# Six buffers for a matmul kernel's split weights, each at its own byte offset from the operand tiles

## The chip, the cores and the metric

The kernel runs on one core of one Trainium2 chip, in one launch. The metric is the time of that core in microseconds (us), as the median of three runs. Times of single instructions are in nanoseconds (ns).

## The reference

One decoder layer over 512 tokens with 2048 features, in float32:

```
mod = silu(c) @ w_ada + b_ada                  # six vectors of 2048
h   = rmsnorm(x, g_mix) * (1 + sc1) + sh1
proj = h @ w_in                                # 2048 x 11344, split in eleven parts
y_a = stick_breaking_attention(q_a, k_a, v_a) @ w_a
y_b = dsa_attention(rope(q_b), rope(k_b), v_b, rope(qi), rope(ki), wi) @ w_b
x   = x + (1 + gt1) * ((sigmoid(g_a) * y_a + sigmoid(g_b) * y_b) @ w_o)
h   = rmsnorm(x, g_ffn) * (1 + sc2) + sh2
u   = causal_conv3(h @ w_up)                   # 2048 x 11264
x   = x + (1 + gt2) * ((silu(u_a) * u_b) @ w_down)
return rmsnorm(x, g_final)
```

Nearly all of the arithmetic is in the products with w_in, w_o, w_up and w_down.

## The kernel before

**A product in three matmuls.** TensorE (PE) multiplies here in a reduced float32 format. To keep float32 accuracy each matrix is held as a high part (the value rounded to that format) and a low part (the rest). `mm3` (lines 142 to 145) makes one product out of three matmuls, high by high (L143), high by low (L144), low by high (L145), into one accumulator in PSUM. A weight tile of 128x1024 comes from memory into one of eight `raw` buffers (`load`). `parts` then splits it: ScalarE (ACT) writes the high part `wh` (L133), VectorE (DVE) writes the low part `wl` (L135). There are three `wh` and three `wl` buffers, and each tile takes the next of its three. `split` (L162, L164) does the same for the operands, which stay for long in the 62 slots `F` of 2048 bytes per partition.

**Two kinds of operand in a matmul.** Each matmul has a stationary operand, 128 columns that an LDWEIGHTS brings into the array beforehand, and a moving operand that is streamed through it, here 256 or 512 columns. The trace writes a matmul as out<-moving,stationary. So `acc<-F,wh 128x256` streams half of an `F` tile through a slice of `wh`, and `att<-wh,F 128x512` streams half of `wh` through a slice of an `F` tile.

**The stages**, with their time in the profile:
- up to about 108 us: most of the indexer's queries, `w_qi`, with `F` moving, 512 columns. Beside it DVE multiplies the first `w_ada` tiles with c. For the first two rounds of this loop `ada_half` borrows two `wl` and two `wh` buffers as landing place.
- to 190 us: `w_va`, with `wh` and `wl` moving; to 237 us a tail of 80 columns (`w_tail`, slices of 80 instead of 128 stationary columns) and three more blocks.
- to 824 us: 31 `unit`s of `w_x`. A unit is one step of Strassen's scheme for a pair of output tiles: seven products of 24 matmuls each, 256 columns, `F` moving and `wh` or `wl` stationary. DVE forms the sums of weight tiles (L233, L237, L275).
- to 1266 us: both attentions, with `w_vb`, `w_a` and `w_b` filled in; to 1445 us `w_o` in units.
- to 2294 us: `w_up`, three blocks plain and 41 units; then `w_down` with `wh` and `wl` moving, 512 columns. Its last stage takes weights that were split into `F` slots ahead of time, so both of its operands are `F` tiles.

**What sets the order.** The program is written with a tile framework. It allots a buffer when a tile is asked for, and a scheduler orders each engine's instructions by dependencies and by when it expects buffers to come free. Each engine then works through its own list and waits only on semaphores. SyncE's queue (SP) issues the weight loads in the order in which it has them.

**Where the buffers lie.** The pool lays tiles of different names one behind the other, in the order in which they are first asked for, each rounded up to a multiple of 32 bytes. In the built program the `F` slots begin at 26912 bytes and lie 2048 bytes apart, so every one begins 288 bytes past a multiple of 2048. The six `wl` and `wh` buffers lie 4096 apart and begin 352 bytes past such a multiple: all six are 64 bytes further on than the operand tiles. The 64 bytes are the small tile `c_col`, which happens to come first in between. A stationary slice of 128 columns is 512 bytes long, and half of an `F` tile 1024, so that the distance between a weight slice and an operand is 64 bytes modulo 512 in all these matmuls.

Of the kernel before, what the change touches and what calls it, by code (L numbers as in the profile page):

```python
# [10 lines left out]
F32 = mybir.dt.float32  # L11
F32R = mybir.dt.float32r
# [64 lines left out]
def block_kernel(ctx: ExitStack, tc: tile.TileContext, A: dict, out: bass.AP):  # L77
# [7 lines left out]
    def nm(s):  # L85
        counter[0] += 1
        return f"{s}_{counter[0]}"

    def t2k(tag, bufs, dt=F32, w=S):
        return sb.tile([P, w], dt, tag=tag, bufs=bufs, name=nm(tag))  # L90

    def slot(dt=F32):

        return t2k("F", SLOTS, dt)
# [14 lines left out]
    stt = nc.vector.scalar_tensor_tensor  # L109


    const = sb.tile([P, 5, P], F32, tag="const", name="const")
    ident, ones, negones, negtri, causal = (const[:, i, :] for i in range(5))
    vec = sb.tile([P, 96 + 2 * KT], F32, tag="vec", name="vec")
# [2 lines left out]
    g_mix, g_ffn = (vec[:, 96 + i * KT : 96 + (i + 1) * KT] for i in range(2))  # L117
    mask = sb.tile([P, 2, P], BF16, tag="mask", name="mask")
    cw = sb.tile([P, 2 * NJ, 4], F32, tag="cw", name="cw")
    eps = sb.tile([P, 1], F32, tag="eps", name="eps")  # L120
    nc.vector.memset(eps, EPS)


    def load(src, w=1024):
# [3 lines left out]

    pins = {}

    def parts(raw, w=1024):
        wh = t2k("wh", 3, F32R, w)
        pins["wh"] = act(wh, raw, AF.Copy)  # L133
        wl = t2k("wl", 3, F32R, w)
        pins["wl"] = tt(wl, raw, wh.bitcast(F32), ALU.subtract)  # L135
        return wh, wl

# [142 lines left out]
        return c1, c2  # L280


    macc = sb.tile([P, 96, 2], F32, tag="macc", name="macc")
    mod = sb.tile([P, 96], F32, tag="mod", name="mod")
    amp = sb.tile([P, 2, KT], F32, tag="amp", name="amp")

    def ada_half(cb, t, half, tag=("raw", 8)):
        raw = t2k(*tag, w=1024)
        nc.sync.dma_start(raw, A["w_ada"][t * P : (t + 1) * P, half * 1024 : (half + 1) * 1024])
        return stt(raw, raw, 1.0, cb[half], ALU.mult, ALU.mult, accum_out=macc[:, t, half : half + 1])  # L290
# [33 lines left out]
        return cb  # L324

    cb = c_spread()
    c_col = sb.tile([P, KT], F32, tag="c_col", name="c_col")
    nc.scalar.dma_start(c_col, A["c_col"])
    act(c_col, c_col, AF.Silu)

# [1 line left out]
    def rms(squares, blocks=range(NQB), bank=outs):  # L332

        total = bank()
        at = slice(blocks[0] * P, (blocks[-1] + 1) * P)
        for b in blocks:
            for i, t in enumerate(squares):
                mm(total[:, b : b + 1], t[:, b * P : (b + 1) * P], ones[:, :1], start=b == blocks[0] and i == 0,
                   stop=i == len(squares) - 1, skip_group_check=True)
        r = sb.tile([P, NQB], F32, tag="r", bufs=2, name=nm("r"))  # L340
        rb = r[:, blocks[0] : blocks[-1] + 1]
        act(rb, total[:, blocks[0] : blocks[-1] + 1], AF.Sqrt, scale=1.0 / D, bias=eps)
        nc.vector.reciprocal(rb, rb)
        wide = t2k("T", 2)
        for b in blocks:
            ts(wide[:, b * P : (b + 1) * P], ident, r[:, b : b + 1], None, ALU.mult)
        yield
        out = bank()
        mm(out[:, at], ones, wide[:, at], start=True, stop=True)
        yield out  # L350
# [16 lines left out]
    for k in range(KT):  # L367
        if k == 6:
            past = t2k("w", 2)[:, :P]
            with behind(pins["load"]):  # L370
                nc.sync.dma_start(const, A["consts"][:, :5])
                nc.sync.dma_start(past, A["consts"][:, 5])
            nc.gpsimd.tensor_copy(mask[:, 0, :], ident)
            nc.gpsimd.tensor_copy(mask[:, 1, :], past)
        t = KT + k
        for half in range(2):
            ada_half(cb, t, half, {0: ("wl", 3), 1: ("wh", 3)}.get(k, ("raw", 8)))
        if not k:
            total = next_x()
        x = xt[k]  # L380
        if k == KT - 1:
            norm = rms([total])
            next(norm)
        ada_end(t, t + 1)
        stt(amp[:, 0, k : k + 1], mod[:, t : t + 1], 1.0, g_mix[:, k : k + 1], ALU.add, ALU.mult)
        h0 = slot(F32R), slot(F32R)
        act(h0[0], x, AF.Copy, scale=amp[:, 0, k : k + 1])
        stt(h0[1], x, amp[:, 0, k : k + 1], h0[0].bitcast(F32), ALU.mult, ALU.subtract)  # L388
        w = prep(A["w_qi"][k], NQ * P)
        for j in range(NQ):  # L390
            mm3(qi_ps[j], cols(w, j), h0, k == 0, k == KT - 1)
            if k == KT - 1 and j == 0:
                rstd = t2k("T", 2)
                act(rstd, next(norm), AF.Copy)
        for _ in range(2 if k == 8 else 1):
            if len(xt) < KT:
                total = next_x()
# [91 lines left out]

    def rope_tables():  # L490
        f0, f1, f2, f3, f123, f23, fr = _turn_parts()
        inv = sb.tile([64, 1], F32, tag="inv", name="inv")
        nc.scalar.dma_start(inv, A["inv_freq"])
        pos = t2k("T", 2, I32)[:64]
        nc.scalar.dma_start(pos, A["positions"].to_broadcast([64, S]))
        turn = [t2k("w", 2)[:64] for _ in range(2)]

        def nearest(o, i, step):
            m = 1.5 * 2.0**23 * step
            ts(o, i, m, m, ALU.add, ALU.subtract)  # L500

        for half in range(2):
            at = slice(half * HALF, (half + 1) * HALF)
            q1, q2 = (t[:, at] for t in turn)
            tmp = sb.tile([P, 5 * HALF], F32, tag="soft", name=nm("soft"))[:64]
            ang, a2, a1, a0, rn = (tmp[:, i * HALF : (i + 1) * HALF] for i in range(5))
            nc.vector.tensor_copy(ang, pos[:, at])
            ts(ang, ang, inv, None, ALU.mult)
            nearest(a2, ang, 2.0**20)
            tt(ang, ang, a2, ALU.subtract)  # L510
            yield
            nearest(a1, ang, 2.0**8)
            tt(ang, ang, a1, ALU.subtract)
            nearest(a0, ang, 2.0**-4)
            tt(ang, ang, a0, ALU.subtract)
            small = ang
            ts(small, ang, fr, None, ALU.mult)
            yield
            stt(small, a0, f123, small, ALU.mult, ALU.add)
            stt(small, a1, f23, small, ALU.mult, ALU.add)  # L520
            stt(small, a2, f3, small, ALU.mult, ALU.add)
            ts(q1, a1, f0, None, ALU.mult)
            stt(q1, a2, f1, q1, ALU.mult, ALU.add)
            yield
            nearest(rn, q1, 1.0)
            tt(q1, q1, rn, ALU.subtract)
            ts(q2, a1, f1, None, ALU.mult)
            stt(q2, a2, f2, q2, ALU.mult, ALU.add)
            nearest(rn, q2, 1.0)
            tt(q2, q2, rn, ALU.subtract)  # L530
            yield
            stt(q1, a0, f0, q1, ALU.mult, ALU.add)
            tt(q1, q1, q2, ALU.add)
            nearest(rn, q1, 1.0)
            tt(q1, q1, rn, ALU.subtract)
            tt(q1, q1, small, ALU.add)
            yield
            nearest(rn, q1, 1.0)
            tt(q2, q1, rn, ALU.subtract)
            ts(q1, q2, 0.25, None, ALU.add)  # L540
            nearest(rn, q1, 1.0)
            tt(q1, q1, rn, ALU.subtract)
            yield
        TWO_PI = float(np.nextafter(np.float32(2 * np.pi), np.float32(0)))
        q1, q2 = turn
        for n, step in enumerate((64, 32)):
            o = t2k("raw", 8, w=1024)
            for i in range(P // step):
                at = slice(step * i, step * i + step)
                act(o[at, :S], q1[:step], AF.Sin, scale=TWO_PI)  # L550
                act(o[at, S:], q2[:step], AF.Sin, scale=TWO_PI if i % 2 else -TWO_PI)
                if i % 2:
                    yield
            save(rope_d[n], o)
# [459 lines left out]
    def norm_late(c1, c2):  # L1014
# [1 line left out]
        c, sq = (c1, c2), (t2k("ta", 2), t2k("sp", 2))  # L1016
        total, rstd = att(), outs()
        wide = t2k("T", 2)
        r = sb.tile([P, NQB], F32, tag="r", bufs=2, name=nm("r"))

        def add_up(t, blocks, first=False):
            for b in blocks:
# [415 lines left out]
        return [fetch(x1t[:, t, b * S : (b + 1) * S]) for b in range(2, 4)]  # L1438

    def finish_tokens(t, xs, s):  # L1440
        r = sb.tile([P, NQB], F32, tag="r", bufs=2, name=nm("r"))
        tt(r[:, :2], s[:, :2], s[:, 2:], ALU.add)
        tt(r[:, 2:3], r[:, :1], r[:, 1:2], ALU.add)
        act(r[:, 3:], r[:, 2:3], AF.Sqrt, scale=1.0 / D, bias=eps)
        nc.vector.reciprocal(r[:, 3:], r[:, 3:])
        for b, x in enumerate(xs):
            if t == NQB - 1 and b < 2:
                act(x, x, AF.Copy, scale=r[:, 3:])
            else:
                stt(x, x, r[:, 3:], g_row[b], ALU.mult, ALU.mult)  # L1450
            nc.sync.dma_start(out[t][:, b * S : (b + 1) * S], x)
# [136 lines left out]
```

## Time and profile before

| | |
|---|---|
| three runs | 2782.76, 2783.45, 2783.63 us |
| median | 2783.45 us |
| profiled execution, its own time | 2759.24 us |
| its span, first to last instruction | 2757.5 us |
| granted TensorE clock, mean | 0.995 |
| ACT busy | 1450.7 us (53%) |
| DMA: bytes moved, mean rate | 550.08 MB, 199 GB/s |
| largest group of DVE: `wl` (L135) | 792 instructions, 952.6 us |

The profiled execution is 24.2 us shorter than the median of the runs. A row of a group of instructions gives how many there were, for how long the engine worked on them, the mean duration of one, and how long the engine stood idle before them. Matmuls overlap in the pipeline: a matmul of 256 columns is shown with some 280 ns, but the next one starts after about 113 ns. What counts for the time is the distance from start to start, called the pace here. It is read from the starts in the timeline, or from the count of matmuls in a window without idle time.

### The profile page before, as it was taken

Reading aid. Unit: us, or ns where it says so; the run is one execution under the profiler, and the core shown is the slowest. Engines: PE = TensorE matmul, PEld = TensorE weight load, DVE = VectorE, ACT = ScalarE, POOL = GpSimd, SP = SyncE. Lnnn points to the kernel's source line nnn. Section 1 sums busy time; section 2 is a strip of 40 time slices with the busy share of each in tenths; the row PEclk is TensorE's granted clock in tenths of the full one; section 3 lists DMA queues with packets and bytes.
Section 4 is the critical chain, followed back from the end, with each engine's and each line's share of the span. In section 5 each row is a group of like instructions: output and inputs, shape, how many; then the busy total and the mean of one; then the engine's idle time right before and its main releaser. Section 6 shows DMA issues by size and latency. Waiting matters only on the chain.

```text
span 2757.5 us, 47708 instructions
## 1 busy us (share of the span) xinstructions
PE 2697.6 (98%) x18704; PEld 2457.7 (89%) x18704; DVE 2411.3 (87%) x3452; ACT 1450.7 (53%) x2045; POOL 315.3 (11%) x519
## 2 busy tenths in 40 slices
PE   8999999999999999999999999999999999999997
PEld 6779999999998777879999999999999998887876
DVE  8978979988887899889879999999999997888886
ACT  4444454455556655434557555555555555546452
POOL 0010000000012011111230000000000000002122
PEclk9999999999999999999999999999999999999998
DMA  9973456756567467865783566666666446569786
GB/s 348 354 254 122 156 181 195 232 176 188 166 195 238 133 206 243 279 213 174 233 269 108 179 176 178 187 177 184 176 179 182 130 131 219 151 176 245 193 256 196
DMA packets 164189, 550.08 MB, mean 199 GB/s; under 512 B 21414, under 2 KB 21798, under 8 KB 163964
## 3 DMA queue, kind: packets, MB, share of 16 engines
q1 hardware_dynamic: 116220, 405.34, 45.9%
q0 software_dynamic: 47152, 141.30, 18.4%
q8 instruction: 147, 2.41, 0.4%
q14 instruction: 78, 0.64, 0.1%
q10 hardware_dynamic: 592, 0.39, 0.1%
HBM read 453.71 MB, written 89.83 MB: 197 GB/s over the span
## 4 chain that ended last, share of the span: by engine, by line
PE 67%; DVE 8%; DMA 5%; issue 4%; ACT 1%; POOL 0%; DVEq 0%; POOLq 0%; ACTq 0%; SPq 0%
PE att L145 10%; PE att L143 10%; PE att L144 10%; PE acc L145 10%; PE acc L143 10%; PE acc L144 10%; DVE wl L135 3%; DMA raw<-in_w_x 1%; DMA raw<-in_w_down 1%; PE acc L722 1%; PE acc L816 1%; PE outs L922 1%; DMA raw<-in_w_o 1%; PE outs L145 1%; PE outs L144 1%
## 5 line engine op out<-in xcount | busy, mean ns | idle before, releaser
L133 ACT ACTIVATE wh<-raw 128x1024 fp32r<-128x1024 f32 (+2 forms) x792 | 828.9, 1053 | 962.2 <-DVE raw L237 179.1
L135 DVE TENSOR_TENSOR wl<-raw,wh 128x1024 fp32r<-128x1024 f32 (+2 forms) x792 | 952.6, 1210 | 126.5 <-ACT wh L133 121.8
L143 PE MATMUL acc<-F,wh 128*128 128x256 f32 (+1 forms) x2464 | 709.1, 290 | 12.8 <-ACT wh L133 7.1
L145 PE MATMUL acc<-F,wl 128*128 128x256 f32 (+1 forms) x2464 | 710.6, 289 | 6.1 <-DVE wl L135 6.1
L144 PE MATMUL acc<-F,wh 128*128 128x256 f32 (+1 forms) x2464 | 710.3, 288 | 0.6 <-DVE F L388 0.4
L143 PE MATMUL att<-F,wh 128*128 128x256 f32 (+1 forms) x2448 | 704.8, 289 | 5.8 <-DVE sp L273 4.5
L145 PE MATMUL att<-F,wl 128*128 128x256 f32 (+1 forms) x2448 | 704.2, 288 | 3.3 <-DVE wl L135 3.0
L144 PE MATMUL att<-F,wh 128*128 128x256 f32 (+1 forms) x2448 | 704.5, 288 | 1.2 <-DVE F L164 1.2
L143 PEld LDWEIGHTS acc<-F,wh 128*128 128x128 f32 x2464 | 463.3, 188 | 29.5 <-ACT wh L133 12.2
L145 PEld LDWEIGHTS acc<-F,wl 128*128 128x128 f32 x2464 | 463.0, 188 | 19.2 <-DVE wl L135 8.5
L143 PEld LDWEIGHTS att<-F,wh 128*128 128x128 f32 x2448 | 460.4, 188 | 19.3 <-ACT wh L133 5.2
L144 PEld LDWEIGHTS acc<-F,wh 128*128 128x128 f32 x2464 | 463.8, 188 | 12.9 <-DVE F L388 1.4
L144 PEld LDWEIGHTS att<-F,wh 128*128 128x128 f32 x2448 | 461.3, 188 | 13.6 <-DVE F L164 4.3
L145 PEld LDWEIGHTS att<-F,wl 128*128 128x128 f32 x2448 | 460.3, 188 | 14.3 <-DVE wl L135 5.0
L290 DVE SCALAR_TENSOR_TENSOR raw<-raw,raw 128x1024 f32<-128x1024 f32 x152 | 182.1, 1217 | 0.0
L143 PE MATMUL att<-wh,F 128*128 128x512 f32 x448 | 178.5, 399 | 0.2 <-ACT wh L133 0.2
L145 PE MATMUL att<-wh,F 128*128 128x512 f32 x448 | 176.3, 394 | 0.0
L144 PE MATMUL att<-wl,F 128*128 128x512 f32 x448 | 176.1, 393 | 0.2 <-DVE wl L135 0.2
L233 DVE TENSOR_TENSOR raw<-raw,raw 128x1024 f32<-128x1024 f32 x80 | 97.4, 1218 | 42.3 <-DMA raw<-in_w_x 24.3
L144 PE MATMUL acc<-wl,F 128*128 128x512 f32 x288 | 114.0, 396 | 2.4 <-DVE wl L135 2.4
L145 PE MATMUL acc<-wh,F 128*128 128x512 f32 x288 | 113.7, 395 | 0.0
L143 PE MATMUL acc<-wh,F 128*128 128x512 f32 x288 | 112.2, 392 | 0.0
(364 smaller groups left out, 3621.3 us busy)
## 6 DMA issues: line engine op xcount, KB each, us to landing
raw<-in_w_up SPq DMA_DIRECT2D x164, 512.0 KB, 4.0
raw<-in_w_ada SPq DMA_DIRECT2D x152, 512.0 KB, 5.2
raw<-in_w_x SPq DMA_DIRECT2D x128, 512.0 KB, 4.3
raw<-in_w_down SPq DMA_DIRECT2D x104, 512.0 KB, 5.3
xd<-F POOLq DMA_DIRECT2D x64, 256.0 KB, 2.5
F<-xd POOLq DMA_DIRECT2D x64, 256.0 KB, 4.7
raw<-in_w_o SPq DMA_DIRECT2D x32, 512.0 KB, 5.1
soft<-in_w_gate SPq DMA_DIRECT2D x32, 512.0 KB, 4.1
```

The lines of the kernel that those rows point to most:

```text
L133: pins["wh"] = act(wh, raw, AF.Copy)
L135: pins["wl"] = tt(wl, raw, wh.bitcast(F32), ALU.subtract)
L143: mm(ps, ah, bh, start=first, stop=False, skip_group_check=not check)
L144: mm(ps, ah, bl, start=False, stop=False, skip_group_check=not check)
L145: return mm(ps, al, bh, start=False, stop=last, skip_group_check=not check)
L233: last_v = tt(s, a21, a22, ALU.add)
L290: return stt(raw, raw, 1.0, cb[half], ALU.mult, ALU.mult, accum_out=macc[:, t, half : half + 1])
L722: mm(dots[:, :W], both[:, b * P : (b + 1) * P], kiR[i][:, :W], start=i == 0, stop=i == 1)
L816: mm(o, negtri if tri else negones, i, start=False, stop=True, skip_group_check=True)
L922: mm(o[:, b * P : (b + 1) * P], vs[kb][:, hd % 4 * HD : (hd % 4 + 1) * HD], pT[b][:, kb * P : (kb + 1) * P], start=kb == 0, stop=kb == b)
```

## The change

The three `wh` and three `wl` buffers become six buffers with names of their own. `parts` takes them in fixed turns: the first call `wh0` and `wl0`, the second `wh1` and `wl1`, the third `wh2` and `wl2`, the fourth the first pair again. At the start of the program all tiles between the operands and the work buffers are asked for in a fixed order, so that small tiles, which existed before at other places, lie between the six buffers. The two `r` tiles, so far two buffers of one name, become two names used in alternation (`small_r`).

```
+    def small_r():
+        counter[0] += 1
+        return sb.tile([P, NQB], F32, tag=f"r{counter[0] % 2}", name=nm("r"))
...
+    amp = sb.tile([P, 2, KT], F32, tag="amp", name="amp")
+    slot()
     eps = sb.tile([P, 1], F32, tag="eps", name="eps")
     nc.vector.memset(eps, EPS)
+    t2k("wh0", 1, F32R, 1024)
+    inv = sb.tile([64, 1], F32, tag="inv", name="inv")
+    t2k("wh1", 1, F32R, 1024)
+    sb.tile([P, NQB], F32, tag="r0", name=nm("r"))
+    t2k("wh2", 1, F32R, 1024)
+    c_col = sb.tile([P, KT], F32, tag="c_col", name="c_col")
+    t2k("wl0", 1, F32R, 1024)
+    sb.tile([P, NQB], F32, tag="r1", name=nm("r"))
+    t2k("wl1", 1, F32R, 1024)
+    sb.tile([P, NQB], F32, tag="m", bufs=2, name=nm("m"))
+    t2k("wl2", 1, F32R, 1024)
...
     def parts(raw, w=1024):
-        wh = t2k("wh", 3, F32R, w)
+        i = turns[0] % 3
+        turns[0] += 1
+        wh = t2k(f"wh{i}", 1, F32R, w)
         pins["wh"] = act(wh, raw, AF.Copy)
-        wl = t2k("wl", 3, F32R, w)
+        wl = t2k(f"wl{i}", 1, F32R, w)
         pins["wl"] = tt(wl, raw, wh.bitcast(F32), ALU.subtract)
         return wh, wl
...
-            ada_half(cb, t, half, {0: ("wl", 3), 1: ("wh", 3)}.get(k, ("raw", 8)))
+            ada_half(cb, t, half, (f"wl{half + 1}", 1) if k == 0 else (f"wh{half + 1}", 1) if k == 1 else ("raw", 8))
```

In the built program the operand tiles then begin 256 bytes past a multiple of 2048 (before: 288), and the distances are these:

| buffer | bytes past a multiple of 2048 | distance from the operand tiles |
|---|---|---|
| any `wh` or `wl`, before | 352 | 64 |
| `wh0`, `wh1`, `wh2`, after | 288, 320, 352 | 32, 64, 96 |
| `wl0`, `wl1`, `wl2`, after | 416, 448, 512 | 160, 192, 256 |

The number of instructions is the same on every engine. The scheduler orders a few of them differently. On SP's queue this is the start of the program (`in_x`, `in_w_qi` and `in_w_ada` are the inputs; `wl` and `wh` as targets are the borrowed buffers). Before:

```order
L289 DMA wl_99<-in_w_ada 128x1024
L289 DMA wl_102<-in_w_ada 128x1024
L359 DMA F_105<-in_x 128x512
L126 DMA raw_115<-in_w_qi 128x896
L126 DMA raw_159<-in_w_qi 128x896
L289 DMA raw_191<-in_w_ada 128x1024
L359 DMA F_142<-in_x 128x512
L289 DMA wh_147<-in_w_ada 128x1024
L289 DMA wh_150<-in_w_ada 128x1024
L289 DMA raw_194<-in_w_ada 128x1024
```

and after:

```order
L309 DMA wl_25_110<-in_w_ada 128x1024
L309 DMA wl_26_113<-in_w_ada 128x1024
L378 DMA F_116<-in_x 128x512
L145 DMA raw_126<-in_w_qi 128x896
L309 DMA wh_36_158<-in_w_ada 128x1024
L309 DMA wh_37_161<-in_w_ada 128x1024
L378 DMA F_153<-in_x 128x512
L145 DMA raw_170<-in_w_qi 128x896
L309 DMA raw_202<-in_w_ada 128x1024
L309 DMA raw_205<-in_w_ada 128x1024
```

The second `w_qi` tile (`raw_159` before, `raw_170` after) now goes out behind two `w_ada` halves and an `x` tile; one `w_ada` half of the next round goes out later.

On DVE's list the second unit of `w_x` shows the kind of move that occurs at a few further places. Before:

```order
L135 TENSOR_TENSOR wl_3818<-raw_3814,wh_3816 128x1024
L237 TENSOR_TENSOR raw_3814<-raw_3814,raw_3776 128x1024
L271 TENSOR_TENSOR raw_3776<-raw_3776,raw_3778 128x1024
L135 TENSOR_TENSOR wl_3852<-raw_3814,wh_3850 128x1024
L135 TENSOR_TENSOR wl_3882<-raw_3782,wh_3880 128x1024
L275 TENSOR_TENSOR raw_3782<-raw_3782,raw_3814 128x1024
```

and after:

```order
L158 TENSOR_TENSOR wl_623_3828<-raw_3824,wh_622_3826 128x1024
L158 TENSOR_TENSOR wl_628_3892<-raw_3792,wh_627_3890 128x1024
L260 TENSOR_TENSOR raw_3824<-raw_3824,raw_3786 128x1024
L294 TENSOR_TENSOR raw_3786<-raw_3786,raw_3788 128x1024
L158 TENSOR_TENSOR wl_625_3862<-raw_3824,wh_624_3860 128x1024
L298 TENSOR_TENSOR raw_3792<-raw_3792,raw_3824 128x1024
```

The low part of one more weight tile (`wl_3882` before, `wl_628` after) is made two sums and one low part earlier, and PE's list in that unit follows it.

More of the change, by code (lines that the diff above doesn't have):

```diff
@@ L119, in block_kernel @@
     cw = sb.tile([P, 2 * NJ, 4], F32, tag="cw", name="cw")
+    macc = sb.tile([P, 96, 2], F32, tag="macc", name="macc")
+    mod = sb.tile([P, 96], F32, tag="mod", name="mod")
+    amp = sb.tile([P, 2, KT], F32, tag="amp", name="amp")
+    slot()
     eps = sb.tile([P, 1], F32, tag="eps", name="eps")
     nc.vector.memset(eps, EPS)
+    t2k("wh0", 1, F32R, 1024)
[9 more added lines that the diff above has]
+    t2k("wl2", 1, F32R, 1024)
     def load(src, w=1024):
@@ L129, in block_kernel @@
     pins = {}
+    turns = [0]
     def parts(raw, w=1024):
-        wh = t2k("wh", 3, F32R, w)
+        i = turns[0] % 3
+        turns[0] += 1
+        wh = t2k(f"wh{i}", 1, F32R, w)
         pins["wh"] = act(wh, raw, AF.Copy)
-        wl = t2k("wl", 3, F32R, w)
+        wl = t2k(f"wl{i}", 1, F32R, w)
         pins["wl"] = tt(wl, raw, wh.bitcast(F32), ALU.subtract)
@@ L280, in unit @@
         return c1, c2
-    macc = sb.tile([P, 96, 2], F32, tag="macc", name="macc")
-    mod = sb.tile([P, 96], F32, tag="mod", name="mod")
-    amp = sb.tile([P, 2, KT], F32, tag="amp", name="amp")
     def ada_half(cb, t, half, tag=("raw", 8)):
@@ L326, in block_kernel @@
     cb = c_spread()
-    c_col = sb.tile([P, KT], F32, tag="c_col", name="c_col")
     nc.scalar.dma_start(c_col, A["c_col"])
@@ L339, in rms @@
                    stop=i == len(squares) - 1, skip_group_check=True)
-        r = sb.tile([P, NQB], F32, tag="r", bufs=2, name=nm("r"))
+        r = small_r()
         rb = r[:, blocks[0] : blocks[-1] + 1]
@@ L491, in rope_tables @@
         f0, f1, f2, f3, f123, f23, fr = _turn_parts()
-        inv = sb.tile([64, 1], F32, tag="inv", name="inv")
         nc.scalar.dma_start(inv, A["inv_freq"])
@@ L1018, in norm_late @@
         wide = t2k("T", 2)
-        r = sb.tile([P, NQB], F32, tag="r", bufs=2, name=nm("r"))
+        r = small_r()
         def add_up(t, blocks, first=False):
@@ L1440, in finish_tokens @@
     def finish_tokens(t, xs, s):
-        r = sb.tile([P, NQB], F32, tag="r", bufs=2, name=nm("r"))
+        r = small_r()
         tt(r[:, :2], s[:, :2], s[:, 2:], ALU.add)
```

## The prediction

> **What bounds the kernel now.** I read the page first: the busy times, and the chain of waits that ended last.
>
> ```profile
> span 2757.5 us, 47708 instructions
> PE 2697.6 (98%) x18704; PEld 2457.7 (89%) x18704; DVE 2411.3 (87%) x3452; ACT 1450.7 (53%) x2045; POOL 315.3 (11%) x519
> PE 67%; DVE 8%; DMA 5%; issue 4%; ACT 1%; POOL 0%; DVEq 0%; POOLq 0%; ACTq 0%; SPq 0%
> ```
>
> PE works for 2697.6 of 2757.5 us, so 59.9 us of idle time is all that any change of waits could win, and the largest single wait is this one (total, times, longest, from the view of waits):
>
> ```profile
> PE acc L143 <- ACT wh L133: 7.1, 2, 6.8
> ```
>
> The rest has to come out of the pace of the matmuls. So the next view is PE alone in windows, in stages where it never stands idle (columns: us, PE busy and matmuls begun, granted clock, DMA share, GB/s), with the first stage ahead.
>
> ```profile
> 0.00:108.00 108.00, 93.17 (x366) 0.98 0.94 338
> 110.00:180.00 70.00, 70.00 (x307) 1.00 0.92 340
> 270.00:370.00 100.00, 100.00 (x851) 1.00 0.50 159
> 490.00:560.00 70.00, 70.00 (x620) 1.00 0.69 227
> 1180.00:1260.00 80.00, 80.00 (x344) 1.00 0.62 203
> 1700.00:1800.00 100.00, 100.00 (x885) 1.00 0.67 178
> 2350.00:2450.00 100.00, 100.00 (x439) 1.00 0.62 175
> ```
>
> Only the first stage is bound by DMA (share 0.94, PE idle for 14.8 us). In all others the granted clock is 1.00, and yet the same matmul of 256 columns takes 100/851 = 117.5 ns in one window, 70/620 = 112.9 and 100/885 = 113.0 ns in others. With 512 columns it is 70/307 = 228 ns, 80/344 = 232.6 and 100/439 = 227.8. Nor does DMA traffic make the slow pace: the slow window has the lowest share, 0.50. A count can miss a record, so I check it by starts in the timeline, first and last row of eight, eight, five, five and five steps:
>
> ```profile
> 299.74 0.28 PE L143 MATMUL acc<-F,wh 128*128 128x256 f32 x1
> 300.69 0.28 PE L145 MATMUL acc<-F,wl 128*128 128x256 f32 x1
> ...
> 1699.75 0.28 PE L143 MATMUL acc<-F,wh 128*128 128x256 f32 x1
> 1700.66 0.28 PE L145 MATMUL acc<-F,wl 128*128 128x256 f32 x1
> ...
> 119.67 0.39 PE L143 MATMUL att<-wh,F 128*128 128x512 f32 x1
> 120.81 0.39 PE L145 MATMUL att<-wh,F 128*128 128x512 f32 x1
> ...
> 1199.81 0.40 PE L143 MATMUL acc<-F,wh 128*128 128x512 f32 x1
> 1200.98 0.39 PE L145 MATMUL acc<-F,wl 128*128 128x512 f32 x1
> ...
> 2709.81 0.39 PE L143 MATMUL acc<-F,F 128*128 128x512 f32 x1
> 2710.94 0.39 PE L145 MATMUL acc<-F,F 128*128 128x512 f32 x1
> ```
>
> These give 0.95/8 = 118.8 and 0.91/8 = 113.8 ns for 256 columns; for 512 columns 228 ns with the weights moving, 234 ns with `F` moving past stationary weights, and 226 ns where both operands are `F` tiles, at distance 0. Nothing here goes below 226 ns for 512 columns or 113 for 256; I call that the floor. The kernel is bound by PE and runs a few per cent above its floor in parts. That is the only thing by which a change of byte offsets can act.
>
> **Does the offset matter at all?** One place before tells: the tail of 80 columns at 190 to 200 us, where the stationary slice moves on by 320 bytes from block to block, so that its distance from `F` changes by 64 modulo 256. Each row below starts a triple of matmuls:
>
> ```profile
> 196.60 0.39 PE L143 MATMUL acc<-F,wh 128*80 128x512 f32 x1
> ...
> 197.28 0.40 PE L143 MATMUL acc<-F,wh 128*80 128x512 f32 x1
> ...
> 197.99 0.40 PE L143 MATMUL acc<-F,wh 128*80 128x512 f32 x1
> ...
> 198.68 0.39 PE L143 MATMUL acc<-F,wh 128*80 128x512 f32 x1
> ...
> 199.36 0.39 PE L143 MATMUL acc<-F,wh 128*80 128x512 f32 x1
> ```
>
> The triples take 0.68, 0.71, 0.69 and 0.68 us: 227, 237, 230 and 227 ns per matmul, with a mean of 230. So the distance matters, one of four is at 10 ns above the floor, two are at it.
>
> For 256 columns the picture is less clean. At the one distance of 64 both paces occur. Going through the timeline I found eight stretches at the slow pace; the first and the last of them, out of eight with 234 us and 1,991 matmuls together:
>
> ```profile
> 264.00:380.00 116.00, 115.24 (x977) 1.00 0.51 165
> ...
> 1572.00:1590.00 18.00, 18.00 (x155) 1.00 0.61 156
> ```
>
> That is 234/1,991 = 117.5 ns, 4.5 ns over the 113.0 of the window at 1700 us, 1,991 × 4.5 = 9.0 us in all. A stretch begins and ends where PE had stood still for a moment; in between the pace holds over different buffers. How weights and operands fall in step after a stall seems to decide it, at an offset that allows both.
>
> **The change part by part.** The numbers of matmuls come from the groups by shape (there are six such lines for 256 columns, three for each of the others, six for `F` moving at 512):
>
> ```profile
> L143 PE MATMUL acc<-F,wh 128*128 128x256 f32 x2240 | 623.3, 278 | 3.4 <-DVE sp L273 2.2 <-DVE F L977 0.5 <-ACT wh L133 0.3
> L143 PE MATMUL att<-wh,F 128*128 128x512 f32 x448 | 178.5, 399 | 0.2 <-ACT wh L133 0.2
> L143 PE MATMUL acc<-wh,F 128*128 128x512 f32 x288 | 112.2, 392 | 0.0
> L143 PE MATMUL outs<-wh,F 128*128 128x512 f32 x96 | 37.6, 392 | 3.1 <-ACT F L436 3.1
> L143 PE MATMUL acc<-F,wh 128*128 128x512 f32 x208 | 79.5, 401 | 9.4 <-ACT wh L133 6.8 <-ACT F L387 1.5 <-ACT F L162 1.2
> ```
>
> *`F` moving, 512 columns.* 208 × 6 = 1,248, less the 366 of the first stage, where DMA hides them: some 880. They leave the distance 64 (234 ns) for six distances. I take the tail's mean of 230 ns: 880 × −4 = −3.5 us. Bounds: all at 226, −7.0; all at the tail's worst of 237, +2.6.
>
> *Weights moving, 512 columns.* (448 + 288 + 96) × 3 = 2,496 at 228 ns. No row shows this form at another distance. The nearest rows are its own 228 and the tail's 230; I take +1 ns, +2.5 us. Bounds: 226, −5.0; 237, +22.5.
>
> *`F` moving, 256 columns.* 2,240 × 6 = 13,440, of which 9.0 us are lost now. Two of the tail's four distances are clean, and a state that one distance sustains should be broken up when the distance changes from weight tile to weight tile; I take half of the loss away, −4.5 us. Bounds: −9.0, and every matmul slow, 13,440 × 4.5 − 9.0 = +51.5 us.
>
> *Fixed turns.* There were three `wh` and three `wl` before, each taking the next; there are three now. A buffer is awaited for as long as before, so no new wait, and PE's waits on `wl` and `wh` stay at a few us. If a turn fell on a buffer still being read where the old pool had another free, the tile would come later by one low part on DVE:
>
> ```profile
> L135 DVE TENSOR_TENSOR wl<-raw,wh 128x1024 fp32r<-128x1024 f32 (+2 forms) x792 | 952.6, 1210 | 126.5 <-ACT wh L133 121.8
> L233 DVE TENSOR_TENSOR raw<-raw,raw 128x1024 f32<-128x1024 f32 x80 | 97.4, 1218 | 42.3 <-DMA raw<-in_w_x 24.3
> ```
>
> That is 1.2 us each time, on an engine that has 13% to spare. Nothing in the numbers; a few of them are inside the range.
>
> *VectorE and ScalarE at new offsets.* The two rows above are the same kind of operation, once over a mix of `raw` and `wh` (1210 ns), once over `raw` alone (1218): the offset does not show in their durations. Zero, covered by PE where it is a few ns.
>
> *The order.* At the start two `w_ada` halves of 512 KB each and an `x` tile go out ahead of the second `w_qi` tile. At the 338 GB/s of the first window the two halves take 1.05 MB / 338 = 3.1 us. The same bytes move in that stage, which DMA bounds; what goes later is offset by what went earlier. Zero, up to +3.1 if PE stands idle for `w_qi`, down to −3.1 if the `w_ada` loop ends sooner. On DVE the one low part that comes earlier in some units moves two sums of 1.2 us each back, while PE has 24 matmuls × 113 ns = 2.7 us of work per product: zero, ±2. The `r` tiles and the borrowed landing places: the same two buffers each as before, zero.
>
> *Sum*: −3.5 + 2.5 − 4.5 = −5.5 us on the profiled execution of 2759.24. The runs shown have a median of 2783.45, 24.2 us more, and no row tells where these lie. If they lie outside what the change touches, the runs go to 2778. But slow stretches that depend on how things fall after a stall may well differ from one execution to the next: 24.2 us would be 5,400 more of the 13,440 at the slow pace. Then half of that goes too, −12.1, and it is 2766. I take the middle, **2772 us**; the forecast's own range is 2764 to 2778.
>
> **The rivals.**
>
> *One or two turns sit at a bad distance for good.* Before, 1,991 of 13,440 matmuls of 256 columns were slow. If one of the six distances sustains the slow pace whatever came before, a third of them are: 4,480 × 4.5 = 20.2 us in place of 9.0, +11 us, 2795; with two turns +31, 2815. It decides from 2,000 slow matmuls on by the profile, or from some 7,400 if the 24.2 us are slow pace as well. For it: one of the tail's four distances is 10 ns slow at 512 columns, and six distances make six chances to hit it. Against it: at 64 bytes 512 columns cost 8 ns more all the time, 256 columns only now and then.
>
> *The pace does not depend on the distance.* The slow stretches at 256 columns come and go with the same addresses, after stalls alone; then the change moves nothing of the 9.0 us, the 3.5 and 2.5 of the sum cancel to 1, and the time is 2780 to 2787. Against it: the tail.
> The Trainium skill, page "SBUF — State Buffer", section "Who interferes with whom", bears on this: TensorE has two read ports, one for the moving operand and one for LDWEIGHTS, independent of each other, and "PE and ACT never wait on anyone". By that rule no distance could cost anything, and the sum would be 0 in place of −5.5; the 234 ns against 226 at the same clock already contradict it in its strict form.
>
> *All six distances are clean.* Every bound on the good side: −9.0 − 7.0 − 5.0 = −21, 2762; and if the 24.2 us go too, 2738. For it: the last stage runs 226 without a break. Against it: the tail's 237 and 230 say that a mere shift is not enough.
>
> **How the numbers follow.** Forecast 0.36; a bad distance 0.30; no dependence 0.18; all clean 0.16. Two runs of this kernel can be told apart from about 0.2%, 5.6 us. The forecast lies beyond that but for its upper end, all clean does wholly, so faster gets 0.50; no dependence and the edge of the forecast give same 0.20; the bad distance is slower, 0.30. The range of 2741 to 2808 leaves out the best corner of all clean and the worse part of two bad turns, with a chance of about 0.2.
>
> **What would show it.** In the profile after: windows of PE in the same stages. The `F`-moving blocks of 512 columns near 1180 us should count 350 or so in 80 us (230 ns) in place of 344; weights moving near 2350 us some 437 in 100 us; `w_up` 885 in 100 us as before, and the window at 270 us between 851 and 885. If one turn is bad, the pace of 256 columns changes with each third weight tile, and windows over many tiles count about 873 in 100 us everywhere. If the distance is nothing, 344 and 439 stay, and slow stretches of the old kind appear at other places. PE's waits on `wl` and `wh` must stay under some 10 us. The forecast is wrong in its cause, whatever the time, if the matmuls keep their paces and the idle time of PE moves by more than 5 us.

## The result and the profile after

The changed kernel takes 2800.61 us (2799.76 to 2804.7) against 2783.45 us (2782.76 to 2783.63) before: 1.0066 of it, with a 95% interval of 1.0043 to 1.0089. It is slower, where faster was forecast; its three runs also lie above every one of the 58 executions of the kernel before that are on record in five sets (2753.75 to 2787.13 us). Its profiled execution, with a span of 2798.8 us, lies 41.3 us above the profiled one of before (2757.5), more than the 17.2 us between the medians; the reason is told with the run that has all six buffers at 64.

The head of the page of the changed kernel:

```profile
span 2798.8 us, 47704 instructions
PE 2744.3 (98%) x18704; PEld 2500.2 (89%) x18704; DVE 2414.1 (86%) x3452; ACT 1455.4 (52%) x2045; POOL 314.7 (11%) x519
```

PE is busy for 98% as before. Its idle time has fallen from 59.9 to 54.5 us and its largest wait is still for `wh`, and no wait that was not there before comes to 1 us:

```profile
PE acc L166 <- ACT wh L156: 8.2, 3, 7.0
```

The time lies in the pace of the matmuls. First one row of before in a long window inside `w_up`, then the changed kernel in that window and in those of the prediction (us, PE busy and matmuls begun, clock, DMA share, GB/s):

```profile
1600.00:2100.00 500.00, 500.00 (x4413) 1.00 0.67 180
```

```profile
270.00:370.00 100.00, 100.00 (x854) 1.00 0.50 159
490.00:560.00 70.00, 70.00 (x598) 1.00 0.67 220
1180.00:1260.00 80.00, 80.00 (x347) 1.00 0.62 202
1600.00:2100.00 500.00, 500.00 (x4257) 1.00 0.64 175
1700.00:1800.00 100.00, 100.00 (x853) 1.00 0.63 172
2350.00:2450.00 100.00, 100.00 (x432) 1.00 0.57 178
```

At 256 columns 500 us held 4,413 matmuls (113.3 ns) and hold 4,257 (117.5 ns). At 512 columns with `F` moving 80 us held 344 matmuls and now hold 347, slightly more; with weights moving 100 us held 439 and now hold 432. The granted clock is 1.00 in all of them.

Which turn pays? The timeline does not number the buffers, but PE goes through the weight tiles in the order of the turns, 24 matmuls to a tile. These are the first matmul of a tile of turn 0, of turn 1, the seventh of turn 1, the first of turn 2, and the first of the next turn 0:

```profile
1709.95 0.28 PE L166 MATMUL acc<-F,wh 128*128 128x256 f32 x1
...
1712.79 0.28 PE L166 MATMUL acc<-F,wh 128*128 128x256 f32 x1
...
1713.50 0.28 PE L166 MATMUL acc<-F,wh 128*128 128x256 f32 x1
...
1715.54 0.28 PE L166 MATMUL acc<-F,wh 128*128 128x256 f32 x1
...
1718.41 0.28 PE L166 MATMUL acc<-F,wh 128*128 128x256 f32 x1
```

Turn 0 (32 and 160 bytes off the operands) takes 2.84/24 = 118.3 ns. Turn 1 (64 and 192) needs 0.71/6 = 118.3 for six matmuls and 2.04/18 = 113.3 from then on, the floor. Turn 2 (96 and 256) takes 2.87/24 = 119.6. So one of three turns is clean and two are slow, and this repeats with every three tiles. In the table below all matmuls of the trace after the first stage are paired in order with the matmuls of the built program, and the distance from start to start is averaged; steps that hold a stop of PE (over 130 ns at 256 columns, over 245 at 512) are left out.

| mean pace in ns | before | after, turn 0 | turn 1 | turn 2 |
|---|---|---|---|---|
| 256 columns, `F` moving | 114.1 | 118.1 | 114.8 | 119.5 |
| 512 columns, `F` moving | 233.2 | 232.6 | 231.9 | 230.2 |
| 512 columns, weights moving | 229.2 | 233.2 | 230.5 | 232.0 |

With some 4,560 matmuls of 256 columns per turn that is 18.3, 3.2 and 24.6 us; weights moving add 2,418 × 2.7 = 6.5 us; `F` moving gives back 1,040 × 1.6 = 1.7 us. The sum is 50.9 us. The steps left out, those with a stop, take 13.7 us less than before (78.2 for 91.9), which fits a PE that goes slower and so waits less; some 3 of the 13.7 us only moved over, as fewer steps hold a stop and more count among the others. All steps of the three forms together took about 40 us longer, of the 41.3 us of the span.

### The profile page after: what moved, and what is told of

The parts are those of the page before. It is cut to its first block, busy times and chain, and to the rows that moved or that the text cites. A ratio compares the mean times of both kernels' runs of the same rounds, so it can differ in the third digit from the quotient of the medians.

```text
span 2798.8 us, 47704 instructions
## 1 busy us (share of the span) xinstructions
PE 2744.3 (98%) x18704; PEld 2500.2 (89%) x18704; DVE 2414.1 (86%) x3452; ACT 1455.4 (52%) x2045; POOL 314.7 (11%) x519
## 5 line engine op out<-in xcount | busy, mean ns | idle before, releaser
L158 DVE TENSOR_TENSOR wl<-raw,wh 128x1024 fp32r<-128x1024 f32 (+2 forms) x792 | 953.6, 1210 | 138.6 <-ACT wh L156 130.7
L168 PE MATMUL acc<-wh,F 128*128 128x512 f32 x288 | 114.1, 396 | 0.0
```

What stands on the lines that cost most here:

```text
L168: return mm(ps, al, bh, start=False, stop=last, skip_group_check=not check)
```

## The experiments

Three theories stood against each other. A: the distance from operand to weight sets the pace of each weight tile. B: each distance is harmless, and what costs is that it changes from tile to tile. C: the fixed turns or the changed order cost the time.

**One distance for all six buffers.** The kernel before, with its rotating buffers and its own order on every engine; only the tiles ahead of the weight buffers differ. At 0:

```
+    c_col = sb.tile([P, KT], F32, tag="c_col", name="c_col")
     eps = sb.tile([P, 1], F32, tag="eps", name="eps")
...
     cb = c_spread()
-    c_col = sb.tile([P, KT], F32, tag="c_col", name="c_col")
     nc.scalar.dma_start(c_col, A["c_col"])
```

> The kernel before with its rotating buffers, c_col moved ahead of the operand tiles, so that all six weight buffers lie at distance 0 instead of 64; every engine's order is that of before. Theory A (the distance of a weight tile from the operands sets the pace of its matmuls, buffer by buffer: in the changed kernel turn 1, at 64 and 192, ran at about 114.5 ns per 256 columns, turn 0, at 32 and 160, at 118, turn 2, at 96 and 256, at 119.5): a distance that is a multiple of 64 is clean, so 113 to 115 ns at 256 columns, at most 229 at 512; 0 to 30 us faster than before. Theory B (the distances are harmless each, it is the change of distance from tile to tile that costs): one distance, so the paces of before, 113 with slow stretches, 228 to 234; within 10 us of before.

At 32, the same with `inv` in the place of `c_col`:

```
     cb = c_spread()
-    c_col = sb.tile([P, KT], F32, tag="c_col", name="c_col")
+    inv = sb.tile([64, 1], F32, tag="inv", name="inv")
...
-        inv = sb.tile([64, 1], F32, tag="inv", name="inv")
         nc.scalar.dma_start(inv, A["inv_freq"])
```

> As the run at 0, with the 32 bytes of the tile inv between operands and weights: all six at 32. Theory A: every matmul as in turn 0, about 118 ns at 256 columns, 13,440 x 4.5 = 60 us at most over the floor; 30 to 60 us slower than before. Theory B: paces and time of before within 10 us.

At 96, and with 16 in place of 8 at 128:

```
-    c_col = sb.tile([P, KT], F32, tag="c_col", name="c_col")
+    c_col = sb.tile([P, KT + 8], F32, tag="c_col", name="c_col")[:, :KT]
```

> The kernel before with c_col 32 bytes longer: all six at 96, order unchanged. Theory A: as turn 2, 119 to 120 ns at 256 columns, 233 at 512; 13,440 x 6 = 80 us over the floor, 50 to 80 us slower than before. Theory B: time of before within 10 us.

> The kernel before with c_col 64 bytes longer: all six at 128, order unchanged. Theory A with multiples of 64 clean: 113 to 115 ns at 256 columns, within 0 to 30 us faster than before. Theory A with a longer period (the tail of 80 columns had shifts by 64 with 227, 237, 230 and 227 ns): 128 may be slow, up to 237 ns at 512 and 118 at 256 columns, up to 70 us slower. Theory B: time of before within 10 us.

Measured against before on the same chip (2777.15 us): at 0 2809.15 us, 1.0127 [1.0092, 1.0162]; at 32 2810.71 us, 1.0134 [1.0098, 1.0169]; at 96 2805.11 us, 1.0104 [1.0059, 1.0149]; at 128 2812.93 us, 1.0138 [1.0102, 1.0174]. The window inside `w_up`, for 0, 32, 96 and 128 in this order, one row of each kernel:

```profile
1600.00:2100.00 500.00, 500.00 (x4169) 1.00 0.64 171
```

```profile
1600.00:2100.00 500.00, 500.00 (x4228) 1.00 0.65 173
```

```profile
1600.00:2100.00 500.00, 500.00 (x4264) 1.00 0.65 174
```

```profile
1600.00:2100.00 500.00, 500.00 (x4216) 1.00 0.64 173
```

These are 119.9, 118.3, 117.3 and 118.6 ns, where 64 gave 113.3. Theory B falls: a single distance that never changes costs as much as the mixture. Theory A stands, but a multiple of 64 is not enough: the expectation at 0 was wrong, and of the one at 128 the second branch came true, that with a longer period. At 96 the pace is below the 119 to 120 ns that were expected from turn 2, whose low part lay at 256. At 0 matmuls of 256 and of 512 columns even part ways. The stage with `F` moving and the stage with weights moving of the run at 0, both at 512 columns:

```profile
1180.00:1240.00 60.00, 59.92 (x264) 1.00 0.65 215
...
2350.00:2450.00 100.00, 100.00 (x443) 1.00 0.56 187
```

100/443 = 225.7 ns by the count, 227.1 over all such matmuls, and 227.5 with `F` moving (before 229.2 and 233.2 counted alike). So 0 is the best distance at 512 columns and the worst measured at 256, where the pace stays at 120 ns from matmul to matmul without a break.

**Turns and order without the distances.** The changed kernel, with the small tiles laid so that all six buffers are at 64 again; its order is that of the changed kernel on every engine.

```
     slot()
+    c_col = sb.tile([P, KT], F32, tag="c_col", name="c_col")
+    t2k("wh0", 1, F32R, 1024)
+    t2k("wl0", 1, F32R, 1024)
+    t2k("wh1", 1, F32R, 1024)
+    t2k("wl1", 1, F32R, 1024)
+    t2k("wh2", 1, F32R, 1024)
+    t2k("wl2", 1, F32R, 1024)
     eps = sb.tile([P, 1], F32, tag="eps", name="eps")
     nc.vector.memset(eps, EPS)
-    t2k("wh0", 1, F32R, 1024)
     inv = sb.tile([64, 1], F32, tag="inv", name="inv")
-    t2k("wh1", 1, F32R, 1024)
...
```

> The changed kernel with its six names, fixed turns and its order on every engine, but the small tiles laid elsewhere so that all six weight buffers lie at 64, as before. Theory A (the distance alone decides): the paces of before, mostly 113 ns at 256 columns with stretches at 118, about 228 and 234 at 512; the time of before within 10 us, so about 25 us faster than the changed kernel. Theory C (the turns or the changed order cost the time): 117 to 118 ns as in the changed kernel, 20 us slower than before.

Measured: 2764.91 us against 2761.19, 1.0017 [0.9984, 1.0050]. Theory C falls: turns and order together cost nothing that can be measured (the interval leaves room for 0.5%). The paces of before are back as well, at 512 columns 233.3 ns with `F` moving and 229.3 with weights moving, so the loss is the distances'. Two windows of this run:

```profile
490.00:560.00 70.00, 70.00 (x620) 1.00 0.66 220
...
1600.00:2100.00 500.00, 500.00 (x4247) 1.00 0.64 174
```

At 64 both paces are there again, 112.9 ns and 117.7; but here the slow one fills the window in which the profiled execution of before was fast throughout. The mean over all matmuls of 256 columns is 115.6 ns here and 114.1 in the trace of before; 1.5 ns for some 13,680 of them are 20 us, about what the two spans differ by (2776.3 and 2757.5 us). Most probably the 24.2 us between before's profile and its median lie there too: single executions at 64 went from 2753.75 to 2786.99 us, in this kernel and in the one before, but only these two have a trace.

**Nine more distances, one pair per turn.** The changed kernel again with other small tiles between the buffers; `wh` and `wl` of a turn lie at the same distance. The first of the three:

```
+    slot()
     amp = sb.tile([P, 2, KT], F32, tag="amp", name="amp")
-    slot()
+    c_col = sb.tile([P, KT], F32, tag="c_col", name="c_col")
+    t2k("wh0", 1, F32R, 1024)
+    t2k("wl0", 1, F32R, 1024)
+    sb.tile([P, NQB], F32, tag="m", bufs=2, name=nm("m"))
+    t2k("wh1", 1, F32R, 1024)
+    t2k("wl1", 1, F32R, 1024)
+    sb.tile([P, NQB], F32, tag="r0", name=nm("r"))
+    sb.tile([P, NQB], F32, tag="r1", name=nm("r"))
+    t2k("wh2", 1, F32R, 1024)
+    t2k("wl2", 1, F32R, 1024)
...
```

> The changed kernel with the same order, the pairs wh0/wl0, wh1/wl1, wh2/wl2 at 192, 256 and 320: a map of three more distances, one per turn. Theory A: each turn has a pace of its own, so a weight tile in three differs. If 64 is the one good distance, all three run at 118 to 120 ns and the time is 20 to 40 us above before; for every turn that runs at 113 the time falls by about 25 us. The changed kernel had wl1 at 192 beside a clean wh1 (115 ns) and wl2 at 256 beside a slow wh2 (118 ns). Theory B (changes of distance cost): all three turns slow alike at 118 or more.

> As the run before, with the pairs at 384, 448 and 480. Theory A: a pace per turn; if -64 (448) mirrors 64, turn 1 runs at 113 to 118 and the others at 118 to 120: 10 to 30 us above before. If no distance but 64 is good, 20 to 40 us above. Theory B: all turns alike.

> As the two before, with the pairs at 160, 224 and 288, all odd multiples of 32. Theory A with weight and operand wanted equal modulo 64: all three slow, 117 to 120 ns, 20 to 40 us above before. Theory A without that: a turn at 113 among them. Theory B: all turns alike.

One execution each: 2802.06, 2804.57 and 2811.2 us. They lie 41 to 50 us above the 2761.19 of before, a little more than expected for three slow turns, and above all of its 13 executions (2782.97 at most). In the window inside `w_up`, in this order:

```profile
1600.00:2100.00 500.00, 500.00 (x4224) 1.00 0.64 173
```

```profile
1600.00:2100.00 500.00, 500.00 (x4237) 1.00 0.65 173
```

```profile
1600.00:2100.00 500.00, 500.00 (x4227) 1.00 0.64 173
```

None reaches 4,413. By turns, worked out as in the table above, the paces at 256 columns are these; the turns differ, as theory A has it.

| distance | 160 | 192 | 224 | 256 | 288 | 320 | 384 | 448 | 480 |
|---|---|---|---|---|---|---|---|---|---|
| ns | 119.9 | 117.4 | 116.8 | 119.6 | 118.4 | 117.7 | 118.8 | 117.7 | 117.6 |

With both parts of a turn at one distance, only 64 of 14 distances has shown the floor. Distances 256 apart have much the same pace, within 0.8 ns (0 and 32 by the runs with one distance for all): 0 and 256 (120.0 and 119.6 ns), 32 and 288 (118.3 and 118.4), 192 and 448 (117.4 and 117.7), 224 and 480 (116.8 and 117.6). 320 is 64 again modulo 256, and has the 117.7 ns of the slow stretches at 64. Its tile comes behind one at 256, a slow one; whether that starts it at the slow pace every time these runs don't tell.

**The pair of the good turn for all.** Turn 1 of the changed kernel had found the floor after six matmuls in each of its tiles, behind a slow turn 0. Is it the pair 64 and 192 that does so (theory D), or did turn 0 hand it a good start (theory E)?

```
+    slot()
+    c_col = sb.tile([P, KT], F32, tag="c_col", name="c_col")
+    t2k("wh0", 1, F32R, 1024)
+    t2k("wh1", 1, F32R, 1024)
+    t2k("wh2", 1, F32R, 1024)
     amp = sb.tile([P, 2, KT], F32, tag="amp", name="amp")
-    slot()
+    t2k("wl0", 1, F32R, 1024)
+    t2k("wl1", 1, F32R, 1024)
+    t2k("wl2", 1, F32R, 1024)
...
```

> The changed kernel with its order, every wh at 64 and every wl at 192, the pair of turn 1, which in the changed kernel came down to 113 ns after six matmuls in each of its tiles, whatever the turn before it ran at. Theory D (that pair has only the fast pace as its steady state): 113 to 114 ns at 256 columns throughout, without stretches at 118, 2745 to 2758 us, 5 to 30 us faster than before. Theory E (turn 1 was fast because turn 0 handed it a good start): both paces in stretches as at 64, 2755 to 2790 us, or 118 throughout and 2800 us.

Measured: 2756.19 us (2750.48 to 2761.73) against 2772.89 (2755.2 to 2784.85), 0.9951 [0.9923, 0.9979]. The window in `w_up`, and ahead of it two in `w_x`; the one at 270 us was slow before (851) and after (854):

```profile
270.00:370.00 100.00, 99.83 (x878) 1.00 0.51 167
490.00:560.00 70.00, 70.00 (x620) 1.00 0.68 219
...
1600.00:2100.00 500.00, 500.00 (x4414) 1.00 0.66 180
```

All three turns have a mean of 113.5 ns; of the slow stretches only short ones are left, none of more than some 30 matmuls. Ten executions scatter over 11 us, where the 18 of before beside them scatter over 30. Theory D stands.

**One bad turn.** The changed kernel with turn 0 moved to 64 and 192, turn 1 there as before, turn 2 left at 96 and 256.

```
+    c_col = sb.tile([P, KT], F32, tag="c_col", name="c_col")
+    t2k("wh0", 1, F32R, 1024)
+    t2k("wh1", 1, F32R, 1024)
     eps = sb.tile([P, 1], F32, tag="eps", name="eps")
     nc.vector.memset(eps, EPS)
-    t2k("wh0", 1, F32R, 1024)
+    t2k("wh2", 1, F32R, 1024)
     inv = sb.tile([64, 1], F32, tag="inv", name="inv")
...
+    sb.tile([P, NQB], F32, tag="m", bufs=2, name=nm("m"))
+    t2k("wl0", 1, F32R, 1024)
+    t2k("wl1", 1, F32R, 1024)
     sb.tile([P, NQB], F32, tag="r0", name=nm("r"))
...
     sb.tile([P, NQB], F32, tag="r1", name=nm("r"))
...
     t2k("wl2", 1, F32R, 1024)
```

> The changed kernel with the same order, turn 0 moved to 64 and 192, turn 2 left at 96 and 256: the price of one bad turn. Theory A (each turn pays for itself): two thirds of the matmuls of 256 columns at 113 to 115 ns, turn 2 at 119.5, 4,480 x 6 = 27 us above the run with all turns at 64 and 192 (2756), so about 2783 us. Theory E (a bad turn spoils the following ones): 2795 us or more, with the good turns at 116 and over.

Measured: 2779.9 us against 2774.19, 1.0021 [0.9999, 1.0042], 3 us below what theory A said. Turns 0, 1 and 2 have means of 114.7, 113.6 and 119.5 ns; in the window:

```profile
1600.00:2100.00 500.00, 500.00 (x4316) 1.00 0.64 176
```

Each turn pays for itself. The tile behind a bad turn needs a few matmuls to settle (114.7 against 113.6), and at 64 and 192 that is all that a change of distance costs.

**A distance for each form.** Buffers 16 columns wider, laid at multiples of 256 from the operands; the stages of 512 columns take them from the start, the units of 256 columns 64 bytes further on. `macc` lies in the room of `cw` to make space.

```
+        wh = t2k(f"wh{i}", 1, F32R, WIDE)[:, at[0] : at[0] + w]
...
+        wl = t2k(f"wl{i}", 1, F32R, WIDE)[:, at[1] : at[1] + w]
...
+    def unit_parts(raw, w):
+        return parts(raw, w, (16, 16))
...
-        product(r1, parts(a11, w), "B11", True)
+        product(r1, unit_parts(a11, w), "B11", True)
```

> The changed kernel with six buffers 16 columns wider, at multiples of 256 from the operands: stages of 512 columns use them from their start (distance 0 modulo 256), the units of 256 columns 64 bytes further on (macc lies in the room of cw to make space). Theory A (each stage runs at the pace of its distance): 227 ns at 512 columns instead of 228 to 234, which is 13 to 15 us less, and 113 or 118 ns at 256 columns as before: 2738 to 2775 us, about 13 us faster than before on the mean of many runs. If 512 columns want 0 modulo 512, half of the buffers stay at 231 and the gain is 7 us.

Measured: 2757.24 us (2751.24 to 2778.96) against 2772.89, 0.9967 [0.9929, 1.0005]. The two stages of 512 columns, and between them the window inside `w_up`:

```profile
1180.00:1240.00 60.00, 60.00 (x266) 1.00 0.68 230
1600.00:2100.00 500.00, 500.00 (x4414) 1.00 0.66 180
2350.00:2450.00 100.00, 100.00 (x442) 1.00 0.58 168
```

The means are 227.6 ns with `F` moving and 227.2 with weights moving, as at 0. `wl0` and `wl2` lie at 256 modulo 512 there and the other four at 0, and their paces do not differ: at 512 columns, 0 and 256 are alike. In the units the same two therefore lie at 320 and `wl1` at 64, all beside a `wh` at 64; the three turns have one mean (115.2 ns), and the 4,414 matmuls are the floor. So 320 does as the partner of 64 what 64 does. The interval touches 1, since at 256 columns 64 brings its two paces and the scatter with it.

**Both.** The same with the units at 64 for `wh` and 192 for `wl`, `wl` 48 columns wider:

```
+    WIDE = {"wh": 1040, "wl": 1072}
...
+        return parts(raw, w, (16, 48))
```

> Both findings in one kernel: stages of 512 columns use the six buffers at multiples of 256 from the operands, the units of 256 columns use wh 64 and wl 192 bytes further on. Theory A with D: 227 ns at 512 columns and 113.4 at 256, so the 13 us of the one come on top of the other; about 2743 us (2738 to 2748), 1.1 to 1.3 per cent faster than before on the same chip, and hardly any scatter between runs. If the two disturb each other at the changes of stage, 2750 to 2757, no better than either alone.

Measured: 2749.93 us (2746.5 to 2752.86) against 2774.19, 0.9910 [0.9886, 0.9933]. This beats both kernels, by 0.9% the one before. It is 7 us short of what was expected, though the paces are nearly those expected, 113.6 and 227.1 to 227.6 ns. In the units two of the low parts lie at 448 and one at 192, without a difference in pace. But PE now stops more in `w_x`; its windows there, to be read beside the 878 and 620 matmuls of the run at 64 and 192:

```profile
270.00:370.00 100.00, 98.80 (x869) 1.00 0.50 163
490.00:560.00 70.00, 68.79 (x604) 1.00 0.64 212
```

From 236 to 835 us PE stands idle for 12.0 us here and for 8.0 in that run, so part of the gain goes into its stops in this stage; what makes it stop more was not tested. Its plain blocks of `w_up` are at distance 0 with 256 columns too, at 120 ns, some 320 matmuls and 2 us.

## Why the prediction was wrong, point by point

- *What bounds the kernel, and by what alone the change could act*: right. PE's waits stayed as they were, and the paces moved the time.
- *Fixed turns, VectorE and ScalarE at new offsets, the order*: costed at nothing, and the run with turns at 64 shows 1.0017 [0.9984, 1.0050]. The `wl` low parts take 953.6 us in place of 952.6. The start, with bounds of ±3.1 us, shows in the first 108 us: 366 matmuls begun before, 370 after, some 1 us.
- *`F` moving, 512 columns*, 234 to 230 ns, −3.5 us: the direction was right, the size too large; 233.2 to 231.6, −1.7 us.
- *Weights moving, 512 columns*, +1 ns and +2.5 us: the direction was right, the size too small; +2.7 ns, 6.5 us.
- *`F` moving, 256 columns*, half of the 9.0 us taken away, −4.5 us: this is the step that failed. It measured +46 us, near the far bound of +51.5. The prediction took the slow stretches for what 64 costs and the 113 ns for the pace that any distance has when left alone. It is the other way round: 113 ns is what 64 allows, and the other distances measured are slow all the time, but for 192, 320 and 448 as the partners of 64. That the state "should be broken up when the distance changes" was an argument without a row behind it.
- *The tail as a sample*: two clean distances out of four at 512 columns and 80 stationary columns were carried over to 256 columns and 128 stationary columns. By the addresses of the built program the tail's slow distance is 0 modulo 256 (mean 234 ns, at the three others 228 to 230). Distance 0, the best at 512 columns and the worst measured at 256, shows that one form does not stand for another.
- *The rival that came true* is the bad distance, with a chance of 0.30: two turns slow for good, as it said. Its price of 4.5 ns over the floor was near (118.1 and 119.5 ns are 4.8 and 6.2 over 113.3). Its +31 us for two turns lie between the 17 us of the medians and the 41 us of the two profiled executions.
- *The rival without dependence* falls: at one clock of 1.00 the same matmul runs at 113.3 or 119.9 ns by the distance alone. The sentence of the Trainium skill that stood behind it ("SBUF — State Buffer", "Who interferes with whom"), "PE and ACT never wait on anyone", does not describe this. *All clean* falls as well.
- *The 24.2 us*: "slow stretches that depend on how things fall after a stall" fits the two traces at 64; single executions at 64 spread over 33 us, at 64 and 192 over 11. What followed from it, that the change would take half of them away, was wrong. And 33 us are 1.2%, so the 0.2% at which two runs were to be told apart was too small, close as the three runs of before lie together (0.9 us).

## What to carry to other kernels

When an engine runs at its full clock without a wait, compare the pace of one instruction form over stages and executions: two paces for one form at one clock are a reason to look at where its operands lie. A fast pace belongs to the place where it was seen, so before moving buffers, ask what the present distance gives; and measure one distance for all buffers before mixing several, since in a mixture the mean hides the good one. Each form of the matmul wants a distance of its own: here 0 or 256 bytes at 512 columns, and 64 for the high and 192 or 448 for the low part at 256 columns.

## What was not expected of the hardware

The pace of a matmul depends on how far its stationary operand lies from its moving one in a partition: at 256 columns 113.3 ns at best and 116.8 to 120.0 elsewhere, at 512 columns 227 to 234. Steps of 32 bytes matter (118.3 ns at 32, 113.3 or 117.7 at 64, 117.9 at 96), steps of 256 hardly (at most 0.8 ns). At 64 two paces, 113 and 117.7 ns, hold for hundreds of microseconds each, and one sequence of addresses can run in either; with `wl` at 192 only the fast one lasted. The position of the buffers by themselves does not show: 64 gave the floor with `F` at 288, 256 and 1664 bytes past a multiple of 2048, and weights at 352 ran at the floor with `F` at 288 and at 120 ns with `F` at 352 (distance 0). Why the distance has this effect, and what starts the one pace or the other at 64, stays open; the runs show only that it is the distance.
